# Products with the states on quarters of TensorE's array, tokens in chunk order, and writes issued by GpSimd

## The chip, the cores and the metric

The kernel runs on one core of a Trainium2 chip. The metric is the time of one execution on the device, in microseconds; several executions are timed, and the median counts. One more execution is recorded by the hardware profiler, and all rows below come from it.

## The reference

A decoder trunk of two layers over 512 tokens with 2048 channels, all in f32. Layer one is a diagonal state-space layer (S5): the input is normalised and multiplied by `s5_w_in` into u and z (2048 channels each); each group of 16 channels of u drives 64 complex states; y is read from the states, goes through gelu, a gate `sigmoid(y @ w_glu + b)` and `silu(z)`, then through `w_out` and a norm into the residual. Layer two is attention with forget gates over 16 heads. The change lies in layer one:

```python
bu = einsum('bsgc,gpc->bsgp', u, b)            # 128 groups of 16 channels, 64 complex states
h_t = abar * h_{t-1} + coef * bu_t             # scan over the 512 tokens
y = einsum('bsgp,gcp->bsgc', h_re, c_re) - einsum('bsgp,gcp->bsgc', h_im, c_im) + d * u
y = gelu(y);  y = y * sigmoid(y @ w_glu + b_glu) * silu(z)
h = x + rmsnorm(y @ w_out)
```

## The kernel before

Large products are made in split precision: each operand is a rounded part (`whi`, `ah`, `BH`) and a rest (`wlo`, `al`, `BL`), and three products of these parts are summed (`mm3`, lines 170 to 172). `proj` makes one block of 128 output channels for all 512 tokens from 48 such instructions. The weights of the next block are loaded while one runs (`ahead`, `piece`, line 145): a load of 512 KB into `wraw` (four buffers), the rounded part on ScalarE, the rest on VectorE. In layer one GpSimd issues these loads.

**Phase A** (`phase_a`) makes u and z, block by block, and between the blocks the state-space work. The order is written out by hand in `order_a`. The 512 tokens are cut into 64 chunks (`NC`) of 8 tokens (`CL`). For each block j of 128 channels, that is 8 groups of 16 channels, there are these steps, and here one block's steps are called a round:

- `ssm_u`: u is scaled by `rstd` on VectorE and written in the order (token in chunk, chunk). Eight DMAs on SP's queue write it to a scratch tensor `ub`, and one reads it back as `U`, with (channel, token in chunk) on the partitions.
- `ssm_tables`, `ssm_kernel`: tables are built from powers of the decay. The table `Et` of the output side makes, with `bb`, the small kernel `kps` (32 columns of the array for each of four pairs of groups). It goes to a scratch tensor `kd`, and eight DMAs on SP's queue read it as the banded matrices `M`, one for each group.
- `ssm_scan`: `xps` is the drive of each chunk from `U`; the scan runs on VectorE over the 64 chunks. Its result is written twice into `Hbd`, the states at the chunk starts, in block-diagonal form: the upper 64 partitions hold the even group and the lower 64 the odd one, each with zeros in the columns of the other.
- `ssm_y`: y of the chunk is the sum of two kinds of product in one bank, `yps`. First the states: for each of four pairs of groups and for the real and the imaginary part, one product of the whole array, 128 rows by 128 columns, with 128 moving columns, half of which are zeros of `Hbd` (line 526). Then the tokens: for each of eight groups and each half of the array's columns, one product with `M`, 128 rows by 64 columns, with 64 moving columns (line 531). Then gelu on ScalarE, and eight DMAs on SP's queue write y to `y_d`.

An f32 product appears in the trace as two instructions, each with its own weight load. The z blocks go to `z_d` by a DMA that ScalarE issues. The input of phase A is `xT`, x transposed on the host, and `rows` spreads `rstd` over the partitions.

**Phase B** reads y and z again, makes the gate with `w_glu`, and multiplies. z is in the order of the tokens and y in the order (token in chunk, chunk), so the product of the two reads z through a transposed view (`nat`, `tk`). Phases C to E hold `w_out`, the norm, and the attention layer.

The framework keeps order on each engine and adds the waits between engines; instructions marked urgent (`high_priority`), the loads of weights among them, are put earlier in an engine's queue.

Of the kernel before, what the change touches and what calls it, by code (L numbers as in the profile page):

```python
# [11 lines left out]
F32 = mybir.dt.float32  # L12
F32R = mybir.dt.float32r
I32 = mybir.dt.int32
AF = mybir.ActivationFunctionType
ALU = mybir.AluOpType
# [4 lines left out]
P = 128  # L21
S = 512
NQ = 4
CL = 8
NC = S // CL
# [39 lines left out]
class Kern:  # L65
# [226 lines left out]
                self.stt(y, a, 1.5, y, ALU.add, ALU.mult)  # L292
        return y

    def rows(self, r, out, pool, tag):

        nc = self.nc
        nb = S // P
        rb = pool.tile([P, nb, P], F32, tag=tag, name="rs_b", bufs=2 if tag == "ev" else 1)
        with self.tc.high_priority():  # L300
            nc.vector.tensor_copy(rb, r.unsqueeze(2).to_broadcast([P, nb, P]))
        ps = self.bank(name="rows")
        for b in range(nb):
            nc.tensor.matmul(ps[:, b * P:(b + 1) * P], lhsT=rb[:, b, :], rhs=self.ident, start=True, stop=True)
        self.act(out, ps)


# [133 lines left out]
    def ssm_kernel(self, j, T):  # L441

        nc, sp = self.nc, self.sp
        ql = NQ * (j % 4)
        qs = slice(NQ * j, NQ * j + NQ)

        Et = T["E"] = sp.tile([P, NQ, CL + 1, 16, 2], F32, tag="Et", name="Et", bufs=2)
        ev = Et.rearrange("p q t c s -> p q t (c s)")
        bc = [P, NQ, CL + 1, 32]
        pe = lambda c: self.AP[:, c, qs, :].unsqueeze(3).to_broadcast(bc)  # L450
        ve = lambda s: self.C4[s][:, ql:ql + NQ].unsqueeze(2).to_broadcast(bc)
        t = sp.tile(bc, F32, tag="tmp", name="ett")
        self.tt(ev, pe(0), ve(0), ALU.mult)
        self.tt(t, pe(1), ve(1), ALU.mult)
        self.tt(ev, ev, t, ALU.add)
        bb = self.bb[j % 2]
        for h in range(2):
            ph = slice(64 * h, 64 * h + 64)
            self.act(bb[ph, :, :, h, :], self.B4[ph, ql:ql + NQ, 1:3])

        kps = self.bank(name="kps")[:, :P]
        for q in range(NQ):
            for c in range(2):
                nc.tensor.matmul(kps[32 * q:32 * q + 32, :], lhsT=bb[:, q, c].rearrange("p g c -> p (g c)"),
                                 rhs=Et[:, q, 0:CL, :, c].rearrange("p t c -> p (t c)"),
                                 start=(c == 0), stop=(c == 1))
        kt = self.ktp[j % 2]
        self.stt(kt[:, 112:P], self.eye16, self.vec["d"][:, j:j + 1], kps[:, :16], ALU.mult, ALU.add)
        self.act(kt[:, P:240], kps[:, 16:])
        kd = self.dp.tile([8, 16, 240], F32, tag="kd", name="kd", bufs=2)  # L470
        nc.sync.dma_start(kd.rearrange("g c n -> (g c) n"), kt)
        M = T["M"] = sp.tile([P, 8, P], F32, tag="M", name="M", bufs=2)
        for g in range(8):
            s = kd[g]
            nc.sync.dma_start(M[:, g, :], bass.AP(s.tensor, s.offset, [[240, 16], [16, 8], [1, P]]))

    def ssm_u(self, j, ps):

        nc, sp = self.nc, self.sp
        u = sp.tile([P, CL, NC], F32, tag="u", name="u", bufs=2)  # L480
        self.tt(u.rearrange("p t k -> p k t"), ps.rearrange("p (k t) -> p k t", t=CL),
                self.rstd.rearrange("p (k t) -> p k t", t=CL), ALU.mult)
        ub = self.dp.tile([16, CL, 8, NC], F32, tag="ub", name="ub", bufs=2)
        for t in range(CL):
            nc.sync.dma_start(ub[:, CL - 1 - t].rearrange("c g k -> g c k"), u[:, t, :])
        U = sp.tile([P, 8, NC], F32, tag="U", name="U", bufs=3)
        nc.sync.dma_start(U, ub.rearrange("c t g k -> (c t) g k"))
        return U

    def ssm_scan(self, j, U, T):  # L490
# [21 lines left out]
        W = sp.tile(bc, F32, tag="Z", name="hw")  # L512
        self.tt(t, rot[:, :, ::2], G[:, :, ::-1], ALU.mult)
        self.tt(W, G, c_, ALU.mult)
        for h in range(2):
            ph = slice(64 * h, 64 * h + 64)
            self.tt(self.Hbd[ph, :, :, h, 1:], W[ph, :, :, :NC - 1], t[ph, :, :, :NC - 1], ALU.add)

    def ssm_y(self, j, U, T):
        nc, sp = self.nc, self.sp  # L520
        yps = self.bank(name="yps").rearrange("p (g k) -> p g k", k=NC)
        H, Et, M = self.Hbd, T["E"], T["M"]
        for q in range(NQ):
            o = yps[:, 2 * q:2 * q + 2, :].rearrange("p g k -> p (g k)")
            for c in range(2):
                nc.tensor.matmul(o, lhsT=Et[:, q, 1:CL + 1, :, c].rearrange("p t c -> p (t c)"),  # L526
                                 rhs=H[:, q, c].rearrange("p g k -> p (g k)"), start=(q == c == 0), stop=False)
        for g in range(2 * NQ):
            for h in range(2):
                ph = slice(64 * h, 64 * h + 64)  # L530
                nc.tensor.matmul(yps[ph, g, :], lhsT=M[:, g, ph], rhs=U[:, g, :],  # L531
                                 start=False, stop=(g == 2 * NQ - 1))

        g_ = sp.tile([P, 8, NC], F32, tag="gy", name="gy", bufs=2)
        self.act(g_, yps, AF.Gelu_apprx_tanh)
        for g in range(8):
            nc.sync.dma_start(self.y_d[j][g].rearrange("c t k -> t c k"), g_[:, g, :])

    def silu2(self, out, z):

# [62 lines left out]
    def phase_a(self, i):  # L603
        nc, K, D, tc = self.nc, self.K, self.D, self.tc
        self.NG = NQ * K
        with ExitStack() as ctx:
# [19 lines left out]
            self.dec = [sp.tile([P, NQ, 2, NC], F32, name=f"dec{b}") for b in range(2)]  # L626
            self.bb = [sp.tile([P, NQ, 2, 2, 16], F32, name=f"bb{b}") for b in range(2)]
            self.ktp = [sp.tile([P, 240], F32, name=f"ktp{b}") for b in range(2)]
            self.Hbd = sp.tile([P, NQ, 2, 2, NC], F32, name="hbd")
            for t in self.dec + self.bb + self.ktp + [self.Hbd]:  # L630
                nc.vector.memset(t, 0.0)
            hk = min(8, K)
            q4 = min(4, K)
# [53 lines left out]
            for n, (c, j) in enumerate(seq):  # L687
# [7 lines left out]
                if (c, j) == ("z", K - 1):  # L695
                    self.z_last = ps
                elif c == "z":
                    z = sp.tile([P, S], F32, tag="zt", name="zt", bufs=2)
                    self.act(z, ps)
                    (nc.sync if n < 2 else nc.scalar).dma_start(self.z_d[j], z)  # L700
                elif c == "u":
                    if j == 0:
                        self.rows(rstd, self.rstd, sp, "gt")
                    U[j] = self.ssm_u(j, ps)
                elif c == "tab":
                    T[j] = self.ssm_tables(i, j)
                elif c == "ker":
                    self.ssm_kernel(j, T[j])
                elif c == "scan":
                    self.ssm_scan(j, U[j], T[j])  # L710
                elif c == "y":
                    self.ssm_y(j, U[j], T[j])
# [30 lines left out]
    def phase_b(self, i, yh, yl):  # L743
# [5 lines left out]
        for f in range(K):  # L749
# [3 lines left out]
            self.tt(z, z, self.rstd, ALU.mult)  # L753
            self.act(t1, z, AF.Tanh, scale=0.5)
            self.stt(z, t1, 1.0, z, ALU.add, ALU.mult)
            self.tt(tk(y), nat(z), tk(y), ALU.mult)
            ps = self.proj(("g", f), yh, yl)
            th = tp.tile([P, S], F32, tag="t1", name="gth", bufs=2)
            self.act(th, ps, AF.Tanh, scale=0.5, bias=hb[:, f:f + 1])
# [326 lines left out]
def layouts(inp):  # L1086

    g = {k: np.ascontiguousarray(np.asarray(v)) for k, v in inp.items()}
    D = g["x"].shape[-1]
# [10 lines left out]
        return v.reshape(K, P).T  # L1100
    a = {}
    a["x"] = g["x"][0]
    a["xT"] = c(g["x"][0].T).reshape(K, P, S)
    a["w_in"] = wt(g["s5_w_in"][0])
    a["w_glu"] = wt(g["s5_w_glu"][0])
    a["w_out"] = wc(g["s5_w_out"][0])
# [47 lines left out]
```

## Time and profile before

| | |
|---|---|
| median of 3 runs | 1796.65 us (1795.36 to 1800.24) |
| profiled execution | 1793.25 us |
| its span, first to last instruction | 1791.5 us |
| TensorE busy in the span | 1772.2 us |
| VectorE, ScalarE, GpSimd busy | 1100.7, 588.9, 345.3 us |

Times in the trace are microseconds from the span's start. PE is TensorE's matmul, PEld its weight load, DVE VectorE, ACT ScalarE, POOL GpSimd, SP the engine that issues most DMAs; a q behind the name is that engine's queue of DMA issues. In a timeline, instructions of one kind that follow each other stand in one row, with their number; a matmul's duration there holds the time to drain, which overlaps the next one, so the pace of a row is read from its start and the start of the row behind it.

### The profile page before, as it was taken

The numbers are of one execution on the slowest core, as the hardware profiler recorded it, in microseconds if no ns is written. First come the engines' busy times: TensorE is split into PE (matmuls) and PEld (weight loads), VectorE is DVE, ScalarE is ACT, GpSimd is POOL, SyncE is SP. The second block draws the span as 40 slices with busy tenths as digits, with TensorE's granted clock in tenths as the row PEclk, the third lists the DMA queues.
The fourth block names the chain that finished last, engine by engine and source line by source line (L and its number), as shares of the span: only waits on it lengthen the run. The fifth ranks groups of instructions, "written<-read, shape, count | busy, mean of one in ns | idle before, by whom it ended". The sixth has DMA issues, their size and how long they took to land.

```text
span 1791.5 us, 24986 instructions
## 1 busy us (share of the span) xinstructions
PE 1772.2 (99%) x9942; PEld 1504.9 (84%) x9942; DVE 1100.7 (61%) x1598; ACT 588.9 (33%) x977; POOL 345.3 (19%) x241
## 2 busy tenths in 40 slices
PE   9999999999999999999999999999999999999997
PEld 6888888888888888898888888888888888988887
DVE  9789899985765622356664666455654556552235
ACT  7333332322544322225332323232332333332221
POOL 1000000000100000012433433334333343300000
PEclk9999999999999999999999999999999999999999
DMA  9545555545644453343333322232233222235332
GB/s 325 152 136 154 142 153 147 150 144 163 213 148 149 160 190 102 98 135 119 95 89 95 90 94 89 93 99 89 89 93 97 91 96 88 89 118 176 98 113 97
DMA packets 141334, 226.49 MB, mean 126 GB/s; under 512 B 53601, under 2 KB 80497, under 8 KB 140961
## 3 DMA queue, kind: packets, MB, share of 16 engines
q1 hardware_dynamic: 126000, 173.79, 31.4%
q0 software_dynamic: 13056, 47.33, 8.3%
q10 hardware_dynamic: 2160, 3.77, 0.6%
q8 instruction: 78, 1.28, 0.3%
q14 instruction: 40, 0.32, 0.1%
HBM read 201.88 MB, written 22.97 MB: 126 GB/s over the span
## 4 chain that ended last, share of the span: by engine, by line
PE 91%; DVE 4%; DMA 2%; SPq 1%; issue 0%; ACT 0%; DVEq 0%; ACTq 0%
PE proj L170 18%; PE proj L172 18%; PE proj L171 18%; PE tok L230 6%; PE tok L231 6%; PE tok L232 6%; PE v L205 3%; PE v L204 3%; PE v L206 3%; PE yps L526 1%; PE t L938 1%; PE yps L531 1%; PE xps L498 1%; DVE al L75 1%; PE btps L424 1%; DVE wlo L151 1%
## 5 line engine op out<-in xcount | busy, mean ns | idle before, releaser
L151 DVE TENSOR_TENSOR wlo<-wraw,whi 128x1024 fp32r<-128x1024 f32 x284 | 421.9, 1487 | 453.5 <-ACT whi L84 453.4
L84 ACT ACTIVATE whi<-wraw 128x1024 fp32r<-128x1024 f32 (+2 forms) x292 | 305.9, 1049 | 848.8 <-PE proj L172 508.2
L147 POOL TENSOR_TENSOR wraw<-wraw,vecs 128x1024 f32<-128x1024 f32 (+1 forms) x128 | 263.0, 2055 | 622.1 <-DMA wraw<-kv_k 254.8
L170 PE MATMUL proj<-BH,whi 128*128 128x512 f32 (+1 forms) x816 | 309.8, 380 | 0.0
L171 PE MATMUL proj<-BH,wlo 128*128 128x512 f32 (+1 forms) x816 | 307.7, 377 | 2.0 <-DVE wlo L151 2.0
L172 PE MATMUL proj<-BL,whi 128*128 128x512 f32 (+1 forms) x816 | 308.0, 377 | 0.5 <-DVE BL L72 0.5
L170 PE MATMUL proj<-ah,whi 128*128 128x512 f32 x768 | 302.2, 394 | 2.1 <-ACT zt L84 1.8
L171 PE MATMUL proj<-ah,wlo 128*128 128x512 f32 x768 | 299.4, 390 | 0.1
L172 PE MATMUL proj<-al,whi 128*128 128x512 f32 x768 | 299.1, 390 | 0.0
L171 PEld LDWEIGHTS proj<-BH,wlo 128*128 128x128 f32 x816 | 153.6, 188 | 30.2 <-DVE wlo L151 2.4
L172 PEld LDWEIGHTS proj<-BL,whi 128*128 128x128 f32 x816 | 153.5, 188 | 29.3 <-DVE BL L72 0.8
L170 PEld LDWEIGHTS proj<-BH,whi 128*128 128x128 f32 x816 | 153.6, 188 | 27.6
L170 PEld LDWEIGHTS proj<-ah,whi 128*128 128x128 f32 x768 | 144.1, 188 | 33.8 <-ACT zt L84 2.2
L171 PEld LDWEIGHTS proj<-ah,wlo 128*128 128x128 f32 x768 | 144.2, 188 | 30.4 <-DVE wlo L151 0.7
L172 PEld LDWEIGHTS proj<-al,whi 128*128 128x128 f32 x768 | 144.2, 188 | 30.3 <-DVE al L75 0.3
L205 PE MATMUL v<-wlo,BH 128*128 128x512 f32 (+2 forms) x320 | 111.4, 348 | 0.0
L204 PE MATMUL v<-whi,BH 128*128 128x512 f32 (+2 forms) x320 | 111.3, 348 | 0.0
L206 PE MATMUL v<-whi,BL 128*128 128x512 f32 (+2 forms) x320 | 111.3, 348 | 0.0
L230 PE MATMUL tok<-whi,BH 128*128 128x512 f32 (+1 forms) x320 | 111.1, 347 | 0.0
L230 PE MATMUL tok<-whi,ah 128*128 128x512 f32 (+1 forms) x320 | 111.0, 347 | 0.0
L232 PE MATMUL tok<-whi,al 128*128 128x512 f32 (+1 forms) x320 | 110.9, 347 | 0.0
L231 PE MATMUL tok<-wlo,ah 128*128 128x512 f32 (+1 forms) x320 | 110.9, 347 | 0.0
(211 smaller groups left out, 2359.9 us busy)
## 6 DMA issues: line engine op xcount, KB each, us to landing
wraw<-w_fox SPq DMA_DIRECT2D x64, 512.0 KB
wraw<-w_in POOLq DMA_DIRECT2D x58, 512.0 KB, 4.3
wraw<-w_glu POOLq DMA_DIRECT2D x32, 512.0 KB, 4.4
wraw<-w_out SPq DMA_DIRECT2D x32, 512.0 KB
wraw<-kv_k SPq DMA_DIRECT2D x32, 512.0 KB
wraw<-w_fo SPq DMA_DIRECT2D x32, 512.0 KB
wraw<-kv_v SPq DMA_DIRECT2D x28, 512.0 KB
M<-kd SPq DMA_DIRECT2D x128, 64.0 KB
```

Of the source, the lines that this page charges most:

```text
L84: self.nc.scalar.activation(out, in_, f, **kw)
L147: (eng or nc.vector).tensor_tensor(raw, raw, scale.unsqueeze(2).to_broadcast(shp), op=ALU.mult)
L151: (eng if eng and scale is None else nc.vector).tensor_tensor(lo, raw, hi, op=ALU.subtract)
L170: mm(ps, lhsT=hi, rhs=xh, start=(k == 0), stop=False)
L171: mm(ps, lhsT=lo, rhs=xh, start=False, stop=False)
L172: mm(ps, lhsT=hi, rhs=xl, start=False, stop=(k == self.K - 1))
L204: nc.tensor.matmul(o, lhsT=xh[k][:, bs], rhs=hi, start=(k == 0), stop=False)
L205: nc.tensor.matmul(o, lhsT=xh[k][:, bs], rhs=lo, start=False, stop=False)
L206: nc.tensor.matmul(o, lhsT=xl[k][:, bs], rhs=hi, start=False, stop=(k == K - 1))
L230: nc.tensor.matmul(ps, lhsT=xh[k][:, bs], rhs=hi, start=(k == 0), stop=False)
L231: nc.tensor.matmul(ps, lhsT=xh[k][:, bs], rhs=lo, start=False, stop=False)
L232: nc.tensor.matmul(ps, lhsT=xl[k][:, bs], rhs=hi, start=False, stop=(k == K - 1))
```

## The change

- `ssm_y`: the products with M come first. The products with the states are cut into quarters of the array: 64 rows (the partitions of an even or an odd group) by 64 columns (four of the eight tokens of a chunk), with 64 moving columns. Even groups go to one bank and odd groups to another, so there are 32 state products in place of 8. gelu is two instructions, one for each bank.
- `ssm_scan`: the states are written once, without the zeros, into `H`.
- `ssm_kernel`: the loop over the real and imaginary part is outside the one over the strips.
- Tokens are in the order (token in chunk, chunk) from the start of phase A: the host writes `xT` so, `rows` writes `rstd` so, and u, z and y need no transposed view on the way. `ub` is written with one DMA and read in pieces.
- The writes of y, and those of z but the first two and the last, are issued by GpSimd.

```diff
--- before.py
+++ after.py
@@ -292,7 +292,7 @@
                 self.stt(y, a, 1.5, y, ALU.add, ALU.mult)
         return y
 
-    def rows(self, r, out, pool, tag):
+    def rows(self, r, out, pool, tag, chunked=False):
 
         nc = self.nc
         nb = S // P
@@ -302,6 +302,8 @@
         ps = self.bank(name="rows")
         for b in range(nb):
             nc.tensor.matmul(ps[:, b * P:(b + 1) * P], lhsT=rb[:, b, :], rhs=self.ident, start=True, stop=True)
+        if chunked:
+            out, ps = out.rearrange("p (t k) -> p t k", t=CL), ps.rearrange("p (k t) -> p t k", t=CL)
         self.act(out, ps)
 
 
@@ -459,8 +461,8 @@
             self.act(bb[ph, :, :, h, :], self.B4[ph, ql:ql + NQ, 1:3])
 
         kps = self.bank(name="kps")[:, :P]
-        for q in range(NQ):
-            for c in range(2):
+        for c in range(2):
+            for q in range(NQ):
                 nc.tensor.matmul(kps[32 * q:32 * q + 32, :], lhsT=bb[:, q, c].rearrange("p g c -> p (g c)"),
                                  rhs=Et[:, q, 0:CL, :, c].rearrange("p t c -> p (t c)"),
                                  start=(c == 0), stop=(c == 1))
@@ -478,13 +480,12 @@
 
         nc, sp = self.nc, self.sp
         u = sp.tile([P, CL, NC], F32, tag="u", name="u", bufs=2)
-        self.tt(u.rearrange("p t k -> p k t"), ps.rearrange("p (k t) -> p k t", t=CL),
-                self.rstd.rearrange("p (k t) -> p k t", t=CL), ALU.mult)
-        ub = self.dp.tile([16, CL, 8, NC], F32, tag="ub", name="ub", bufs=2)
-        for t in range(CL):
-            nc.sync.dma_start(ub[:, CL - 1 - t].rearrange("c g k -> g c k"), u[:, t, :])
+        tk = lambda v: v.rearrange("p (t k) -> p t k", t=CL)
+        self.tt(u[:, ::-1], tk(ps), tk(self.rstd), ALU.mult)
+        ub = self.dp.tile([8, 16, CL, NC], F32, tag="ub", name="ub", bufs=2)
+        nc.sync.dma_start(ub.rearrange("g c t k -> (g c) t k"), u)
         U = sp.tile([P, 8, NC], F32, tag="U", name="U", bufs=3)
-        nc.sync.dma_start(U, ub.rearrange("c t g k -> (c t) g k"))
+        nc.sync.dma_start(U, ub.rearrange("g c t k -> (c t) g k"))
         return U
 
     def ssm_scan(self, j, U, T):
@@ -512,29 +513,33 @@
         W = sp.tile(bc, F32, tag="Z", name="hw")
         self.tt(t, rot[:, :, ::2], G[:, :, ::-1], ALU.mult)
         self.tt(W, G, c_, ALU.mult)
-        for h in range(2):
-            ph = slice(64 * h, 64 * h + 64)
-            self.tt(self.Hbd[ph, :, :, h, 1:], W[ph, :, :, :NC - 1], t[ph, :, :, :NC - 1], ALU.add)
+        self.tt(self.H[:, :, :, 1:], W[:, :, :, :NC - 1], t[:, :, :, :NC - 1], ALU.add)
 
     def ssm_y(self, j, U, T):
         nc, sp = self.nc, self.sp
-        yps = self.bank(name="yps").rearrange("p (g k) -> p g k", k=NC)
-        H, Et, M = self.Hbd, T["E"], T["M"]
+
+
+        yps = [self.bank(name=f"yps{h}")[:, :NQ * NC].rearrange("p (q k) -> p q k", k=NC) for h in range(2)]
+        H, Et, M = self.H, T["E"], T["M"]
+        half = [slice(64 * x, 64 * x + 64) for x in range(2)]
         for q in range(NQ):
-            o = yps[:, 2 * q:2 * q + 2, :].rearrange("p g k -> p (g k)")
+            for h in range(2):
+                for x in half:
+                    nc.tensor.matmul(yps[h][x, q], lhsT=M[:, 2 * q + h, x], rhs=U[:, 2 * q + h, :],
+                                     start=(q == 0), stop=False)
+        for q in range(NQ):
             for c in range(2):
-                nc.tensor.matmul(o, lhsT=Et[:, q, 1:CL + 1, :, c].rearrange("p t c -> p (t c)"),
-                                 rhs=H[:, q, c].rearrange("p g k -> p (g k)"), start=(q == c == 0), stop=False)
-        for g in range(2 * NQ):
-            for h in range(2):
-                ph = slice(64 * h, 64 * h + 64)
-                nc.tensor.matmul(yps[ph, g, :], lhsT=M[:, g, ph], rhs=U[:, g, :],
-                                 start=False, stop=(g == 2 * NQ - 1))
+                for n, x in enumerate(half):
+                    for h, ph in enumerate(half):
+                        nc.tensor.matmul(yps[h][x, q],
+                                         lhsT=Et[ph, q, 1 + 4 * n:5 + 4 * n, :, c].rearrange("p t c -> p (t c)"),
+                                         rhs=H[ph, q, c], start=False, stop=(q == NQ - 1 and c == 1))
 
         g_ = sp.tile([P, 8, NC], F32, tag="gy", name="gy", bufs=2)
-        self.act(g_, yps, AF.Gelu_apprx_tanh)
+        for h in range(2):
+            self.act(g_[:, h::2], yps[h], AF.Gelu_apprx_tanh)
         for g in range(8):
-            nc.sync.dma_start(self.y_d[j][g].rearrange("c t k -> t c k"), g_[:, g, :])
+            nc.gpsimd.dma_start(self.y_d[j][g].rearrange("c t k -> t c k"), g_[:, g, :])
 
     def silu2(self, out, z):
 
@@ -626,8 +631,8 @@
             self.dec = [sp.tile([P, NQ, 2, NC], F32, name=f"dec{b}") for b in range(2)]
             self.bb = [sp.tile([P, NQ, 2, 2, 16], F32, name=f"bb{b}") for b in range(2)]
             self.ktp = [sp.tile([P, 240], F32, name=f"ktp{b}") for b in range(2)]
-            self.Hbd = sp.tile([P, NQ, 2, 2, NC], F32, name="hbd")
-            for t in self.dec + self.bb + self.ktp + [self.Hbd]:
+            self.H = sp.tile([P, NQ, 2, NC], F32, name="hst")
+            for t in self.dec + self.bb + self.ktp + [self.H]:
                 nc.vector.memset(t, 0.0)
             hk = min(8, K)
             q4 = min(4, K)
@@ -697,10 +702,10 @@
                 elif c == "z":
                     z = sp.tile([P, S], F32, tag="zt", name="zt", bufs=2)
                     self.act(z, ps)
-                    (nc.sync if n < 2 else nc.scalar).dma_start(self.z_d[j], z)
+                    (nc.sync if n < 2 else nc.gpsimd).dma_start(self.z_d[j], z)
                 elif c == "u":
                     if j == 0:
-                        self.rows(rstd, self.rstd, sp, "gt")
+                        self.rows(rstd, self.rstd, sp, "gt", True)
                     U[j] = self.ssm_u(j, ps)
                 elif c == "tab":
                     T[j] = self.ssm_tables(i, j)
@@ -753,7 +758,7 @@
             self.tt(z, z, self.rstd, ALU.mult)
             self.act(t1, z, AF.Tanh, scale=0.5)
             self.stt(z, t1, 1.0, z, ALU.add, ALU.mult)
-            self.tt(tk(y), nat(z), tk(y), ALU.mult)
+            self.tt(y, z, y, ALU.mult)
             ps = self.proj(("g", f), yh, yl)
             th = tp.tile([P, S], F32, tag="t1", name="gth", bufs=2)
             self.act(th, ps, AF.Tanh, scale=0.5, bias=hb[:, f:f + 1])
@@ -1100,7 +1105,7 @@
         return v.reshape(K, P).T
     a = {}
     a["x"] = g["x"][0]
-    a["xT"] = c(g["x"][0].T).reshape(K, P, S)
+    a["xT"] = c(g["x"][0].T.reshape(D, NC, CL).transpose(0, 2, 1)).reshape(K, P, S)
     a["w_in"] = wt(g["s5_w_in"][0])
     a["w_glu"] = wt(g["s5_w_glu"][0])
     a["w_out"] = wc(g["s5_w_out"][0])
```

## Rows read from the trace of the kernel before

**Rows 1.** The page: busy time of the engines, and TensorE's granted clock in 40 slices.

```profile
PE 1772.2 (99%) x9942; PEld 1504.9 (84%) x9942; DVE 1100.7 (61%) x1598; ACT 588.9 (33%) x977; POOL 345.3 (19%) x241
...
PEclk9999999999999999999999999999999999999999
```

**Rows 2.** Busy time by stretch: engine busy (instructions), clock, DMA share, GB/s.

```profile
66.00:434.00 368.00, 366.98 (x2870) 308.43 (x2868) 320.06 (x359) 115.84 (x195) 27.06 (x52) 1.00 0.52 146
434.00:607.00 173.00, 173.00 (x767) 143.26 (x764) 103.20 (x116) 73.19 (x90) 16.21 (x31) 1.00 0.52 170
```

**Rows 3.** Timeline of TensorE, 113.9 to 119.3 us: start, us, engine, line, operation, tiles.

```profile
114.36 0.71 PE L464 MATMUL kps<-Et,bb 128*32 128x128 f32 x16
115.01 2.15 PE L526 MATMUL yps<-hbd,Et 128*128 128x128 f32 x16
117.08 1.15 PE L531 MATMUL yps<-U,M 128*64 128x64 f32 x32
118.07 1.10 PE L498 MATMUL xps<-U,BT 128*64 128x64 f32 x32
119.10 0.50 PE L170 MATMUL proj<-ah,whi 128*128 128x512 f32 x1
```

**Rows 4.** Timeline of TensorE, 129.8 to 136 us.

```profile
130.12 1.04 PE L424 MATMUL btps<-ident,Bt 128*128 128x128 f32 x8
130.99 2.04 PE L526 MATMUL yps<-hbd,Et 128*128 128x128 f32 x16
132.97 1.15 PE L531 MATMUL yps<-U,M 128*64 128x64 f32 x32
134.05 0.69 PE L464 MATMUL kps<-Et,bb 128*32 128x128 f32 x16
```

**Rows 5.** Timeline of TensorE from 399.6 us on; idle time and its releaser in brackets.

```profile
399.67 0.69 PE L464 MATMUL kps<-Et,bb 128*32 128x128 f32 x16
...
413.31 2.04 PE L526 MATMUL yps<-hbd,Et 128*128 128x128 f32 x16
415.29 0.45 PE L531 MATMUL yps<-U,M 128*64 128x64 f32 x8
416.51 1.09 PE L531 MATMUL yps<-U,M 128*64 128x64 f32 x16 [0.77 <-DMA M<-kd]
...
418.25 0.69 PE L464 MATMUL kps<-Et,bb 128*32 128x128 f32 x16
```

**Rows 6.** Timeline of TensorE, only what began or ran from 114.30 to 114.42 us.

```profile
114.36 0.35 PE L464 MATMUL kps<-Et,bb 128*32 128x128 f32 x4
```

**Rows 7.** Timeline of SP's queue, 396 to 418 us: start, us in all, line, tiles.

```profile
403.36 2.42 SPq L537 DMA_DIRECT2D y_d<-gy  x4
...
408.86 0.40 SPq L471 DMA_DIRECT2D kd<-ktp  x1
410.65 5.38 SPq L475 DMA_DIRECT2D M<-kd  x8
```

**Rows 8.** Groups of VectorE by line and shape, 66 to 607 us: busy us, mean ns.

```profile
L72 DVE TENSOR_TENSOR hbd<-hw,ht 64x504 f32<-64x504 f32 x32 | 21.7, 678 | 0.8
...
L72 DVE TENSOR_TENSOR u<-proj,rstd 128x512 f32<-128x512 f32 x16 | 17.3, 1081 | 1.9 <-PE proj L172 1.9
L72 DVE TENSOR_TENSOR yld<-zld,yld 128x512 f32<-128x512 f32 x14 | 16.0, 1141 | 0.5
...
L72 DVE TENSOR_TENSOR hw<-G,rot 128x512 f32<-128x512 f32 x16 | 11.0, 685 | 0.0
```

**Rows 9.** A group of GpSimd by line and shape, 0 to 900 us.

```profile
L145 POOL DMA_DIRECT2D wraw<-w_in x58 | 30.7, 530 | 382.9 <-DVE wlo L151 340.5 <-DMA xin<-xT 17.9 <-DVE scr L72 11.8
```

**Rows 10.** Timelines of GpSimd (first row) and of ScalarE (second), 200 to 232 us.

```profile
201.09 0.53 POOL L145 DMA_DIRECT2D wraw<-w_in  x1 [4.85 <-DVE wlo L151]
...
230.70 1.05 ACT L84 ACTIVATE whi<-wraw 128x1024 fp32r<-128x1024 f32 x1
```

**Rows 11.** Weight loads from GpSimd (line 145), 66 to 607 us.

```profile
DMA to landing us min/median/max: 3.8/4.3/7.2
```

## The prediction

> **What bounds the kernel now.** I read the page's busy shares first, then the busy time by stretch, then the timeline of TensorE around one round of the state-space stage, then the queues. [...]
>
> [...] In a round with a z projection before it, TensorE runs kps (114.36), the products of the states (115.01), those of the tokens with M (117.08), xps (118.07), and is back at a projection at 119.10 [rows 3]. In the other kind the order is btps, states, M, kps [rows 4]. From the first state product to the instruction after the last M product it is 118.07 - 115.01 = 3.06 us in the one and 134.05 - 130.99 = 3.06 us in the other. Sixteen of these are 49 us: that is what the change works on. One round differs: at 415.29 the M products stop for loads of M, and the part takes 418.25 - 413.31 = 4.94 us, 1.88 more [rows 5].
>
> **What the products cost, and what quarters may do.** An f32 product stands in the trace as two instructions. On the whole array with 128 columns streamed, btps takes (130.99 - 130.12)/8 = 0.109 us for each [rows 4], so 64 columns alone would take about 0.054. The state products take (132.97 - 130.99)/16 = 0.124, some with a change of shape in it. The M products, on 64 columns of the array with 64 streamed, take (118.07 - 117.08)/32 = 0.031 [rows 3]: half of 0.054 and a little, so the two halves of the array run side by side. kps, on strips of 32 columns with 128 streamed, takes 0.65/16 = 0.041 against 0.109, so strips overlap there as well, although the loop sends four instructions in a row to one strip.
>
> *Removed:* 16 instructions on the whole array (8 products), half of whose moving columns are zeros. *Added:* 32 products, 64 instructions, of 64 rows, 64 columns and 64 streamed. If the four quarters run side by side as the two halves do, a set of four takes what a pair of M instructions takes, 0.99/16 = 0.062 us, and 16 sets take 0.99 us. Changes of shape: the M part takes 0.99 us when the next work has its shape and 134.05 - 132.97 = 1.08 when it has not [rows 4], so about 0.09 for a change. After the edit M and states each end in one: 1.08 + 1.08 = 2.16 us. Round by round, kps to projection was 4.74 us and becomes 0.65 + 1.08 + 1.08 + 1.03 = 3.84. The saving is 0.90 us, and 16 × 0.90 = 14.4 us.
>
> No row of before shows an instruction on 64 rows, so its pace is bounded. Best: sets at 0.062 with no cost of shape, M and states 0.99 each, 1.08 saved, 17.3 us in all. Worst: no overlap at all, 64 × 0.054 = 3.46 us. I take the four side by side: halves and strips both overlap in this trace, and even and odd groups write to a bank each.
>
> How fast instructions can start also matters: 64 in 0.99 us is one each 0.015 us. The window that ends at 114.42 holds four kps instructions that began at 114.36 or later [rows 6], so starts can follow each other within about 0.02 us. That is a burst; whether it holds over 64 no row shows. [...]
>
> **The other edits.** *M ahead of the states:* in the late round M must now be there at 413.31, not 415.29 [rows 5]. But kd waited on SP's queue behind eight y writes and was issued at 408.86, although its kps had begun at 399.67 [rows 5] and takes 0.65; M's eight loads were issued from 410.65 on over 5.4 us [rows 7]. With y off that queue, kd can go out a few us after kps, some 5 us earlier, and M is there by about 411 to 413. I count the 1.88 us as gained; bounds: 0, or, with M no earlier, 2 us more lost, since the state products no longer cover it. *ub:* eight writes become one and U is read in pieces instead; U is loaded two rounds ahead, and the one us that TensorE is not busy in the stretch [rows 2] is the wait for M. *Order of kps:* strips overlap already; four at full pace would be 16 × 0.109/4 = 0.44 us plus a change of shape, at best 0.12 × 16 = 1.9 us; I take 0. *VectorE:* u 1081 ns and yld 1141 ns go to about 685, as the same shape without a transposed order takes, and two H sums of 678 become one [rows 8]: some 24 us less, none of it on the path, since TensorE is full in both stretches [rows 2]. If that cover were gone, it would be worth at most the few us of TensorE's waits. *ScalarE:* one gelu becomes two of half the size, at most as much again; its banks are next needed a projection later. The transposed write of rstd happens once.
>
> *y and z on GpSimd:* per round eight issues of y and mostly one of z. A weight load, with 128 rows like a write of y, costs 530 ns to issue [rows 9], so a round adds 9 × 0.53 = 4.8 us, plus a wait for gelu, in front of the weight loads queued behind. Who waits for those: whi, then wlo, then TensorE. There are four buffers, so the load issued at 201.09 is converted only after the three others, at 230.70 [rows 10], and it lands 4.3 us after issue, at most 7.2 [rows 11]. That leaves some 22 us, or, if the weight loads of the next product are queued strictly behind y, a few us. I count 0. On the last round y goes out after gelu as before, and SP is free for the loads of yld sooner.
>
> **The sum.** 14.4 + 1.9 = 16.3 us. The profiled execution took 1793.25 us (span 1791.5), so it would be 1777. The median shown is 1796.65, 3.4 above it; there the sum gives 1780.4, and I predict 1780. Some 0.3% (5.4 us) is what a measurement of this kernel can tell from no change.
>
> **Rivals.**
> *Two at a time.* Rows 0 to 63 and 64 to 127 of the same columns exclude each other, or the 0.031 us of an M instruction is the pace of issue and not of two halves. Then the states take 64 × 0.031 = 1.98 us plus 0.09, with M 3.15 against 3.06: 1.4 us lost over 16 rounds, 1.9 gained in the late one: 1796. For: kps and M both come near 0.03 to 0.04. Against: the four starts [rows 6]. Chance 0.16.
> [...] Chance 0.05. [...]
> *Quarters one by one (slower).* Place: the state products alone; price: 3.46 + 1.08 + 0.09 = 4.63 against 3.06, 1.57 × 16 = 25 us lost, 1.9 gained: 1820. It decides as soon as one of the 64 takes over 0.031 us. Against it: halves overlap with the same kind of instruction. Chance 0.06.
> *Weights late behind y.* It decides where GpSimd's extra 4.8 us a round, with the wait for gelu, grows past what the buffers leave, which needs about 1 us an issue and a strict order; 3 us lost in each second round is 24 us, 16 gained: about 1804. Chance 0.05.
>
> **How the numbers follow.** Four side by side has 0.68; its own range is 1775 (best shape costs and kps at its best) to 1786 (M's wait not gained, and 0.25 us more a round for shapes). Below it nothing is left. Two at a time reaches to 1797, and up to there 0.89 is held; the range 1775 to 1797 holds about 0.85 once I allow for mis-sized terms. Faster by over 0.3%: 0.68 + 0.05 = 0.73. Same: 0.16. Slower: 0.11.
>
> **What would show it.** In the timeline, states after M, 64 instructions in about 1.0 us; M and states 2.1 to 2.2 us in all rounds, the one at 413 without a wait; kps still 0.6 us; nine issues a round on GpSimd with no TensorE wait for wlo. VectorE's busy time falls by some 24 us without an effect of its own. It is wrong if the 64 take 2 us or more, if M's loads show among TensorE's waits, or if weights do.

## The result and the profile after

The changed kernel takes 1786.9 us, median of five runs (1782.97 to 1789.21), against 1796.05 of the kernel before on the same chip: ratio 0.9946, 95% interval 0.9935 to 0.9958. That is 9.2 us gained where 16.3 were forecast, inside the range. The profiled execution took 1786.9 us, its span 1785.1, so in the two profiles the spans differ by 6.4 us.

First the page of the changed kernel: busy time of the engines and the granted clock [rows 1].

```profile
PE 1762.5 (99%) x10710; PEld 1493.7 (84%) x10710; DVE 1078.4 (60%) x1582; ACT 590.1 (33%) x993; POOL 430.0 (24%) x382
...
PEclk9999999999999999999999999999999999999999
```

TensorE has 768 instructions more (16 rounds × 48) and is busy for 9.7 us less; VectorE 22.3 us less, GpSimd 84.7 us more. The timeline of TensorE in a round with a z projection [rows 3], and the busy time by stretch [rows 2], show where:

```profile
114.79 0.67 PE L466 MATMUL kps<-Et,bb 128*32 128x128 f32 x16
115.39 1.15 PE L528 MATMUL yps<-U,M 128*64 128x64 f32 x32
116.47 1.19 PE L534 MATMUL yps<-hst,Et 64*64 64x64 f32 x64
117.59 1.15 PE L499 MATMUL xps<-U,BT 128*64 128x64 f32 x32
118.67 0.50 PE L170 MATMUL proj<-ah,whi 128*128 128x512 f32 x1
```

```profile
66.00:422.00 356.00, 354.21 (x3644) 294.88 (x3643) 303.87 (x343) 116.53 (x211) 106.38 (x182) 1.00 0.54 153
...
805.00:870.00 65.00, 59.17 (x412) 55.75 (x411) 37.98 (x75) 21.51 (x42) 19.21 (x10) 0.95 0.26 82
```

The M part takes 116.47 - 115.39 = 1.08 us and the 64 state instructions 117.59 - 116.47 = 1.12, one each 0.0175 us: 2.20 us in place of 3.06. This repeats in all rounds to within 0.01 us, but for the last one. The round that waited for M [rows 5] now has no wait. From the start of the product that spreads `rstd` (65.51 us before, 66.34 after) to the end of the last round (434.02 and 421.77), the state-space stage shrinks from 368.51 to 355.43 us, by 13.1.

The last row of the windows is new to the argument: between 805 and 870 us, in the attention layer, whose code the change does not touch, TensorE is busy for 59.17 of 65 us, and the mean granted clock is 0.95. In the kernel before, the same stretch of the program lies some 12 us later and loses less:

```profile
817.00:882.00 65.00, 60.74 (x445) 57.22 (x444) 39.99 (x77) 23.92 (x45) 20.89 (x11) 1.00 0.29 90
```

Of the 12.25 us by which TensorE is ahead at the end of the state-space stage, 11.5 are left at the first value product (tile `v`; 829.45 and 817.95), 7.96 at the cumulated gates (873.19 and 865.23), and 6.4 at the end of the span. Where the last 1.6 us go was not traced.

The other edits in the profile: groups of VectorE by line and shape [rows 8], and one of GpSimd, 66 to 607 us.

```profile
L72 DVE TENSOR_TENSOR u<-proj,rstd 128x512 f32<-128x512 f32 x16 | 11.0, 686 | 3.3 <-PE proj L172 3.3
L72 DVE TENSOR_TENSOR hst<-hw,ht 128x504 f32<-128x504 f32 x16 | 10.9, 683 | 0.6
```

```profile
L542 POOL DMA_DIRECT2D y_d<-gy x128 | 76.7, 606 | 15.9 <-ACT gy L84 4.3 <-issue 3.9 <-DMA y_d<-gy 3.5
```

### The profile page after: what moved, and what is told of

The parts are those of the page before. It is cut to its first block, busy times and chain, and to the rows that moved or that the text cites. A ratio compares the mean times of both kernels' runs of the same rounds, so it can differ in the third digit from the quotient of the medians.

```text
span 1785.1 us, 26466 instructions
## 1 busy us (share of the span) xinstructions
PE 1762.5 (99%) x10710; PEld 1493.7 (84%) x10710; DVE 1078.4 (60%) x1582; ACT 590.1 (33%) x993; POOL 430.0 (24%) x382
## 3 DMA queue, kind: packets, MB, share of 16 engines
q0 software_dynamic: 18192, 55.01, 10.3%
## 4 chain that ended last, share of the span: by engine, by line
PE 92%; DVE 5%; DMA 2%; issue 1%; ACT 0%; SPq 0%; POOL 0%; DVEq 0%; ACTq 0%; POOLq 0%
PE proj L170 18%; PE proj L172 18%; PE proj L171 18%; PE tok L232 6%; PE tok L231 6%; PE tok L230 6%; PE v L204 3%; PE v L205 3%; PE v L206 3%; PE yps L534 1%; PE t L943 1%; PE yps L528 1%; PE xps L499 1%; DVE wlo L151 1%; PE btps L426 1%; DVE al L75 1%
```

## The experiments

Each ratio is against the kernel before, run beside it on the same chip (its medians were 1795.2 to 1796.3 us); "stage" is the time from the `rstd` product to the end of the last round in the profiled execution (368.5 before, 355.4 changed). A time is the median of four or five runs of the kernel, of twelve and eleven for the two under 1.

### 1. The products alone, and the rest alone

`q_only` is the kernel before with the product change only: quarters, two banks, M first, states written once, two gelu. Queues, token order and kps are as before. `rest_only` is the changed kernel with the old products, whole array with `Hbd` and one bank; the ends of its edit, with the old loops of `ssm_y` between them:

```diff
-        self.tt(self.H[:, :, :, 1:], W[:, :, :, :NC - 1], t[:, :, :, :NC - 1], ALU.add)
+        for h in range(2):
+            ph = slice(64 * h, 64 * h + 64)
+            self.tt(self.Hbd[ph, :, :, h, 1:], W[ph, :, :, :NC - 1], t[ph, :, :, :NC - 1], ALU.add)
...
-        for h in range(2):
-            self.act(g_[:, h::2], yps[h], AF.Gelu_apprx_tanh)
+        self.act(g_, yps, AF.Gelu_apprx_tanh)
```

> Only the products: states on quarters in two banks, M first, one H; tokens, queues and the order of kps as in the kernel before. Theory 1 (the gain is the shorter state products): a round's M and state part falls from 3.06 to about 2.2 us, in all rounds but the late one, some 13 us by the end of the state-space stage; y is still ahead of kd on SP's queue, so the late round waits for M for 2 to 4 us. Time 0.4 to 0.7% under before. Theory 2 (the gain is mostly the freed queues and vector work): under 0.2% better than before.

> All of the change but the products: states as before, on the whole array with the zeros, in one bank, ahead of M. Theory 1: the 16 rounds keep 3.06 us each, only the wait for M in the late round goes, so the time is within 0.2% of before. Theory 2: most of the 9 us are here, 0.4% better or more.

Measured: q_only 1796.21 us, ratio 1.0001 (0.999 to 1.0011); stage 366.2. rest_only 1792.39, ratio 0.9988 (0.9979 to 0.9997); stage 365.6. In q_only the products are as short as in the changed kernel, 1.08 and 1.12 us, but three rounds wait for M: the M part takes 2.70, 7.68 and 3.00 us there. So the trace bears out the mechanism of theory 1, with more waits than it allowed for, although the time is the one that theory 2 gave. Timeline of TensorE in the second of these, and of SP's queue ahead of it:

```profile
405.39 0.34 PE L527 MATMUL yps<-U,M 128*64 128x64 f32 x4
409.00 1.59 PE L527 MATMUL yps<-U,M 128*64 128x64 f32 x20 [3.28 <-DMA M<-kd]
411.85 0.48 PE L527 MATMUL yps<-U,M 128*64 128x64 f32 x4 [1.25 <-DMA M<-kd]
412.65 0.48 PE L527 MATMUL yps<-U,M 128*64 128x64 f32 x4 [0.32 <-DMA M<-kd]
```

```profile
395.70 2.51 SPq L541 DMA_DIRECT2D y_d<-gy  x4
398.39 0.32 SPq L487 DMA_DIRECT2D U<-ub  x1
398.75 2.43 SPq L541 DMA_DIRECT2D y_d<-gy  x4
401.28 0.40 SPq L471 DMA_DIRECT2D kd<-ktp  x1
403.07 5.08 SPq L475 DMA_DIRECT2D M<-kd  x8
```

The eight writes of y stand ahead of kd, and M is still on its way when its products begin. The x20 instructions of the second row take (411.85 - 1.25 - 409.00)/20 = 0.08 us each where 0.034 is usual, and the granted clock was 0.56 on average from 409 to 412 us. So neither part saves much alone: the shorter products are eaten by the queue, and a free queue has only the one wait of before to remove.

### 2. Which of the queue's loads matters

`queues_back` is the changed kernel with y on SP and z on ScalarE again; u still goes out in one write. `q_and_y` is q_only with y and z on GpSimd, and still eight writes of `ub` and the old token order. The edit of queues_back (that of q_and_y is its reverse, on q_only):

```diff
-            nc.gpsimd.dma_start(self.y_d[j][g].rearrange("c t k -> t c k"), g_[:, g, :])
+            nc.sync.dma_start(self.y_d[j][g].rearrange("c t k -> t c k"), g_[:, g, :])
...
-                    (nc.sync if n < 2 else nc.gpsimd).dma_start(self.z_d[j], z)
+                    (nc.sync if n < 2 else nc.scalar).dma_start(self.z_d[j], z)
```

> The changed kernel with the writes of y issued by SP again and those of z by ScalarE; u still goes through one write and the products stay on quarters. Theory: y ahead of kd on SP's queue makes M late, and that eats the shorter products. Then kd and M are issued some 4 to 5 us later in the late rounds, TensorE waits for M in at least one of the last three rounds, 3 us or more in all (with the clock lowered behind a long wait perhaps more), the state-space part ends 3 to 9 us later than in the changed kernel (421.8 us), and the time is 1790 to 1796 us. Rival: the eight writes of ub were what blocked SP; then the stage ends by about 423 and the time stays at 1786 to 1788.

> The kernel before with the quarters (M first, two banks, states written once, two gelu) and with y and z issued by GpSimd, but with the eight writes of ub and the token order of before. Theory (y's queue is what matters): no long wait for M, the state-space part ends by 421 to 424 us, the time is 1784 to 1789 us, as the changed kernel's. Rival (the eight writes of ub, or the transposed reads on VectorE, count too): M is late again, the part ends at 427 or later and the time is 1791 to 1796 us.

> The changed kernel once more, on the same chip as the three others, so that they can be compared with it; 1785 to 1789 us. If the wait at the z0 product depends on which of the two engines begins first, it may be about 2 us this time in place of 3.9, with no fall of the clock there, and the span 3 us shorter; if the chain itself got longer, it is 3.9 again.

Measured: queues_back 1787.84 us, ratio 0.9959 (0.9947 to 0.9972), stage 360.8; q_and_y 1784.68, ratio 0.9936 (0.9924 to 0.9949), stage 355.8; the changed kernel once more 1786.22, ratio 0.995 (0.9936 to 0.9963), stage 355.5. In queues_back the last two rounds wait for M, and the M part takes 4.16 and 3.50 us there; its timeline:

```profile
402.82 0.80 PE L528 MATMUL yps<-U,M 128*64 128x64 f32 x20
406.37 0.68 PE L528 MATMUL yps<-U,M 128*64 128x64 f32 x12 [2.74 <-DMA M<-kd]
406.98 1.65 PE L534 MATMUL yps<-hst,Et 64*64 64x64 f32 x64
```

The stage is 5.3 us longer there, as the theory of y's queue said; the time, 1.6 us longer, is less than it said (1790 to 1796), and the two intervals overlap. With y gone, the eight writes of `ub` cost nothing: q_and_y has the stage of the changed kernel within 0.4 us and its time within the interval. So, beside the quarters, only the move of y and z is needed. No run moves one of the two alone; the queue in the rows above holds y and no z. The single write of `ub`, the token order and the shorter work on VectorE add nothing that shows.

### 3. The order of the quarters

`by_quarter` sends the same 32 state products, one quarter's eight after the other's:

```diff
-        for q in range(NQ):
-            for c in range(2):
-                for n, x in enumerate(half):
-                    for h, ph in enumerate(half):
+        for n, x in enumerate(half):
+            for h, ph in enumerate(half):
+                for q in range(NQ):
+                    for c in range(2):
```

> The changed kernel with the 32 state products sent quarter by quarter, eight in a row (16 instructions) to each. If TensorE takes work for a free quarter from behind waiting instructions, as it seems to do with the strips of kps, the states stay at about 1.1 us a round and the time is that of the changed kernel. If instructions start in the order in which they are sent, each quarter runs alone: 64 at 0.055 to 0.06, some 3.6 us a round, 40 us more in all, slower than before.

Measured: 1821.55 us, ratio 1.0144 (1.0131 to 1.0157). Timeline of TensorE:

```profile
115.44 1.15 PE L528 MATMUL yps<-U,M 128*64 128x64 f32 x32
116.53 3.50 PE L534 MATMUL yps<-hst,Et 64*64 64x64 f32 x64
119.96 0.74 PE L499 MATMUL xps<-U,BT 128*64 128x64 f32 x18
```

The states take 119.96 - 116.53 = 3.43 us, 0.0536 each: near the price of "no overlap at all" in the prediction (3.46), and its slower rival to 2 us (1820). So the gain comes from four quarters at work at once, and here that needed an order that goes round them: 1.12 us for the states in place of 3.43.

That 3.43 is so near to 3.46 is luck. Within one quarter an instruction starts each 0.060 us, so 64 without any overlap would take 3.84; but two quarters overlap where one takes over from the other. The rows are windows of TensorE's timeline, inside the first quarter (117.16 to 117.18 us) and at the border to the second (117.46 to 117.48):

```profile
117.00 0.40 PE L534 MATMUL yps<-hst,Et 64*64 64x64 f32 x4
117.30 0.40 PE L534 MATMUL yps<-hst,Et 64*64 64x64 f32 x7
```

Four starts in 0.18 us become seven. In all 16 rounds the second quarter begins 0.774 to 0.778 us after the first, where sixteen starts of the first alone would need more than 0.95: three of its sixteen are still to come. So, by these starts, three waiting instructions are passed, but not the fifteen and more that this order would need. It fits that kps overlapped for the most part in the kernel before, with four in a row to each strip: 16 instructions in 0.61 to 0.65 us, where one after the other at the 0.109 of btps would be 1.74 [rows 3, 4].

### 4. States ahead of M

`states_first` swaps the two loops of `ssm_y` back, with the quarters kept:

```diff
-            for h in range(2):
-                for x in half:
-                    nc.tensor.matmul(yps[h][x, q], lhsT=M[:, 2 * q + h, x], rhs=U[:, 2 * q + h, :],
-                                     start=(q == 0), stop=False)
-        for q in range(NQ):
...
-                                         rhs=H[ph, q, c], start=False, stop=(q == NQ - 1 and c == 1))
+                                         rhs=H[ph, q, c], start=(q == c == 0), stop=False)
+        for q in range(NQ):
+            for h in range(2):
+                for x in half:
+                    nc.tensor.matmul(yps[h][x, q], lhsT=M[:, 2 * q + h, x], rhs=U[:, 2 * q + h, :],
+                                     start=False, stop=(q == NQ - 1))
```

> The changed kernel with the states ahead of M again. If a change of shape costs 0.09 us, M is followed by xps in its own shape in the 8 rounds with a z projection: 0.8 us less; the last round's wait for M (1.1 us in the changed kernel) is covered by the states. 1 to 2 us better in the state-space stage, which the time can hardly tell. If M first was needed for the overlap or for the bank, it gets slower instead.

> The changed kernel with the state products ahead of those with M, once more, as the base of the other two: 1780 to 1784 us.

Measured: 1782.13 us, ratio 0.9925 (0.9913 to 0.9936), and again 1782.42, ratio 0.9919 (0.9906 to 0.9933); stage 352.2 both times. It beats both kernels. Timeline of TensorE in a round with a z projection:

```profile
115.94 1.19 PE L529 MATMUL yps<-hst,Et 64*64 64x64 f32 x64
117.06 1.15 PE L535 MATMUL yps<-U,M 128*64 128x64 f32 x32
118.04 1.10 PE L499 MATMUL xps<-U,BT 128*64 128x64 f32 x32
119.08 0.50 PE L170 MATMUL proj<-ah,whi 128*128 128x512 f32 x1
```

M takes 118.04 - 117.06 = 0.98 us, 0.10 less, since xps behind it has its shape, and xps itself takes 119.08 - 118.04 = 1.04, 0.05 less by the unrounded times. There are seven such rounds. In the eight with btps ahead, btps keeps its 0.97. The last round does not wait for M, because the states cover 1.12 us of its way. That is 7 × 0.15 + 1.12 = 2.2 of the 3.2 us by which the stage is shorter; the other 1.05 us are the stall told at the end of this document, which is gone as well.

### 5. What was lost behind the stage

The second profile of the changed kernel (`after_again`) has the same stage within 0.1 us, but a span of 1781.2 us, 3.9 shorter. Most of the difference, some 3.2 us, is in the first z product of the attention layer (z0). Another 0.7 us were lost at 810 us: behind a wait of 1.69 us the granted clock was 0.50 from 810 to 813 us in the first profile, and it did not fall there in the second. TensorE at z0 in the first profile, and in the second:

```profile
857.03 0.28 PE L170 MATMUL proj<-BH,whi 128*128 128x256 f32 x1
860.90 0.58 PE L171 MATMUL proj<-BH,wlo 128*128 128x256 f32 x1 [3.60 <-DVE wlo L151]
861.28 0.41 PE L172 MATMUL proj<-BL,whi 128*128 128x256 f32 x1
861.50 0.41 PE L170 MATMUL proj<-BH,whi 128*128 128x256 f32 x1
...
864.27 0.29 PE L171 MATMUL proj<-BH,wlo 128*128 128x256 f32 x1
864.40 0.28 PE L172 MATMUL proj<-BL,whi 128*128 128x256 f32 x1
```

```profile
856.85 0.28 PE L170 MATMUL proj<-BH,whi 128*128 128x256 f32 x1
858.80 0.39 PE L171 MATMUL proj<-BH,wlo 128*128 128x256 f32 x1 [1.67 <-DVE wlo L151]
859.02 0.28 PE L172 MATMUL proj<-BL,whi 128*128 128x256 f32 x1
859.14 0.28 PE L170 MATMUL proj<-BH,whi 128*128 128x256 f32 x1
```

What VectorE and GpSimd do at that moment, first profile:

```profile
857.92 2.92 DVE L151 TENSOR_TENSOR wlo<-wraw,whi 128x1024 fp32r<-128x1024 f32 x1
...
857.87 1.90 POOL L147 TENSOR_TENSOR wraw<-wraw,vecs 128x1024 f32<-128x1024 f32 x1 [5.45 <-DMA wraw<-w_fox]
```

and second:

```profile
857.53 1.22 DVE L151 TENSOR_TENSOR wlo<-wraw,whi 128x1024 fp32r<-128x1024 f32 x1
...
857.51 2.98 POOL L147 TENSOR_TENSOR wraw<-wraw,vecs 128x1024 f32<-128x1024 f32 x1 [6.02 <-DMA wraw<-w_fox]
```

GpSimd's multiply of the next weights and VectorE's `wlo` begin within 0.05 us of each other, and one of them is stretched by nearly the length of the other: 2.92 in place of 1.22, or 2.98 in place of 1.90. Which one loses decides whether TensorE waits 3.87 us from start to start or 1.95. Behind the longer wait the clock falls: from 861.28 to 864.27 TensorE's instructions follow each other at 0.214 us in place of 0.120, and the windows give a granted clock of 0.50:

```profile
857.00:861.00 4.00, 0.41 (x4) 0.20 (x2) 3.97 (x5) 0.63 (x1) 1.90 (x1) 0.98 0.03 11
861.00:864.00 3.00, 3.00 (x14) 3.00 (x15) 0.45 (x1) 0.00 (x0) 0.00 (x0) 0.50 0.55 173
```

That costs 14 × 0.094 = 1.3 us more. (In q_only the clock fell behind a wait of 2.05 us as well, to 0.53 on average from 870 to 873 us.) Over the eleven profiles that share this code, the start of `wlo` against that of the multiply goes with which of the two is stretched; why, no run shows. In six VectorE keeps its 1.22 us: there `wlo` begins between 184 ns ahead of the multiply and 12 ns behind it (both of the kernel before, rest_only, q_only, after_again, states_first), and TensorE's wait is 1.86 to 2.17 us from start to start. In five GpSimd keeps its 1.90 us: there `wlo` begins 51 to 121 ns behind (the changed kernel's first, q_and_y, queues_back, by_quarter, sf_again), and the wait is 3.65 to 3.87.

`no_scale` leaves GpSimd's multiply out (the attention layer's weights are used unscaled); `sf_vec5` and `sf_vec` are states_first with VectorE multiplying, for five products or for all. The first edit below is that of no_scale, the second that of sf_vec5; sf_vec has `self.stream(items)` there:

```diff
-            if scale is not None:
+            if scale is not None and eng is None:
...
-        self.stream([w + (nc.gpsimd,) for w in items])
+        self.stream([w if n < 5 else w + (nc.gpsimd,) for n, w in enumerate(items)])
```

> The changed kernel without GpSimd's multiply of the attention layer's weights (the pieces are used unscaled, so the output is another one). Theory: that multiply, when it begins before VectorE's wlo, holds wlo up (2.92 in place of 1.22 us), and this with the granted clock that falls behind the wait is what was lost between 805 and 870 us. Then all wlo of that stretch take about 1.2 us, the wait at the z0 product falls from 3.9 to about 2 us, the clock does not fall there, and the time is 1781 to 1784 us. Rival (the loss has nothing to do with the two engines; the wait comes from the chain of the forget gate on VectorE): the wait and the time stay, 1786 to 1788 us.

> States ahead of M, and VectorE in place of GpSimd multiplies the weights of the first five products of the attention layer (up to the one behind z0). Theory: two engines that hold each other up cost 4 us or more between 800 and 870 us, even in the run in which the wait at z0 was short. Then no wlo there takes over 1.4 us, the wait at z0 goes to 1 us or less, and the time is 1777 to 1780 us. Rival: each piece now passes VectorE twice, behind the chain of the forget gate, so wlo is late at z0 all the same, by 3 us or more with a fall of the clock behind it; then 1781 to 1786.

> As the one with the first five, but VectorE multiplies the weights of all products of the attention layer. Theory: TensorE is never without work from 870 to 1600 us, VectorE is busy for 58% of that stretch there and gets some 100 us more, so it makes no difference to the one with five: 1777 to 1780. Rival: with VectorE fuller, softmax or wlo come late and TensorE waits in that stretch: over 1785.

Measured: no_scale 1777.39 us, ratio 0.9901 (0.9888 to 0.9915), 8.8 us below the changed kernel beside it, with the same stage (355.1). TensorE's busy time from 805 to 870 us is

```profile
805.00:870.00 65.00, 63.94 (x462) 60.51 (x462) 33.88 (x86) 25.69 (x49) 1.29 (x1) 1.00 0.28 95
```

against 59.17 and, in the second profile, 60.67 us of the changed kernel. The wait at z0 is gone altogether, not only down to 2 us as expected; presumably the weights are also there earlier without the multiply, which was not traced. So this run shows what the multiply costs in all, and the pair of profiles above shows what the collision alone does.

Giving the multiply to VectorE takes the collision away only in sf_vec (from 795 to 870 us each `wlo` takes 1.22 to 1.29 us there, and in sf_vec5 one still takes 2.67), and makes another wait: sf_vec5 1787.81 us, ratio 0.9951 (0.9938 to 0.9963); sf_vec 1789.23, ratio 0.9958 (0.9945 to 0.997); 5.4 and 6.8 us slower than states_first beside them, and for sf_vec5 above both ranges that I expected. Timeline of TensorE in sf_vec5:

```profile
808.52 1.94 PE L797 MATMUL hT<-ident,al 128*128 128x128 f32 x8 [4.23 <-DVE al L75]
...
847.88 0.74 PE L170 MATMUL proj<-BH,whi 128*128 128x512 f32 x1 [4.09 <-DVE ke L75]
```

The instructions that TensorE waits for on VectorE now come later than before: the first of these waits was 1.69 us in sf_again and the second is new. A lower granted clock stands behind each (0.50 from 808.5 to 812 us, 0.58 from 848 to 852), and together they cost more than the collision.

A second profile of the kernel before asked whether the long wait at z0 belongs to the change:

> The kernel before, unchanged, for a second profile of it. Theory: the wait at the z0 product is chance, about 2 or about 3.8 us whichever kernel runs, with a fall of the clock behind the long one; then this profile shows one of the two values, the state-space part takes 368.5 us from rows to its end within 0.5, and if the long wait is there the span is 1794 to 1796. Rival: the long wait belongs to the changed kernel; then it is 1.9 again and the span is 1791 to 1792.

Its span is 1795.7 us, 4.2 longer than the first, but not for z0: the wait there is 2.17 us from start to start, as short as in the first (1.86). The late round took longer, 4.53 us for its M part against 2.97, with a granted clock of 0.57 behind it, from 420 to 424 us, and the stage 371.6 us, not the 368.5 that I expected. So the kernel before has a luck of its own, at M.

## Why the prediction was right, and where it was off

- *Four quarters at once:* right. 64 instructions took 1.12 us; forecast was 1.08. Behind the first, the sets of four start each 0.060 us; forecast was 0.062. Two at a time (1.98 us) and one by one (3.46) are out, and by_quarter shows about what the latter would have looked like.
- *Whether close starts hold over 64:* they do, one each 0.0175 us with the start and the change of shape in it, in every round. The 0.05 that the prediction adds to 0.68 stands for a slower pace of starts; no run shows such a pace for instructions that go round four quarters at a granted clock of 1.00.
- *Changes of shape:* M and states take 2.20, forecast 2.16. Not counted was the change between btps and M: btps takes 130.68 - 129.71 = 0.97 us after and 0.87 before [rows 4]:

```profile
129.71 1.04 PE L426 MATMUL btps<-ident,Bt 128*128 128x128 f32 x8
130.68 1.15 PE L528 MATMUL yps<-U,M 128*64 128x64 f32 x32
```

  That is 0.10 lost in each second round. The sum also left xps at 1.03, the value behind M; behind the states it takes 118.67 - 117.59 = 1.08, 0.05 lost in seven rounds. The new order of kps, counted at nothing, gives 0.60 for 0.61 to 0.65. Summed over the stage in the two traces, btps is 0.74 us longer, xps 0.19 (one xps near the end got shorter) and kps 0.52 shorter: 0.4 us lost in all.
- *M's wait:* the 1.88 us of the late round were gained as forecast. But a round that did not wait before now does, the last one:

```profile
418.44 1.04 PE L528 MATMUL yps<-U,M 128*64 128x64 f32 x28
420.38 0.34 PE L528 MATMUL yps<-U,M 128*64 128x64 f32 x4 [0.91 <-DMA M<-kd]
420.64 1.19 PE L534 MATMUL yps<-hst,Et 64*64 64x64 f32 x64
```

  The M part takes 420.64 - 418.44 = 2.20 us, 1.12 too many. (In `after_again` the M part takes 2.70 there.) The step "M ahead of the states" named this price (2 us "since the state products no longer cover it") for the late round only. states_first shows that the new order of the two products was itself worth less than nothing.
- *Weights late behind y:* out. A write of y costs GpSimd 606 ns, more than the 530 counted, and TensorE waits for no weights in the stage.
- *VectorE's and ScalarE's work:* VectorE's busy time fell by 22.3 us (forecast some 24), and q_and_y, which keeps the transposed reads, is no slower.
- *The sum* is where the prediction was off, in its size. Over the stage it nearly holds: 16 × 0.86 + 1.88 - 1.12 = 14.5 us from M and states, less the stall of 1.05 told below and the 0.4 of btps, xps and kps, is 13.1, and 13.1 are there. But the prediction took it that what the stage gains arrives at the end, because TensorE is full behind it [rows 2]. That window ended at 607 us. From 805 to 870 TensorE waits for VectorE, and what it loses there is not a constant: two executions of the same program differ by 3.9 us in their spans. In the profiles of before the wait at z0 is the short one, twice; in the changed kernel the long one came in one of two, and in all profiles with the quarters whose attention layer is untouched, in five of eight. So part of the shortfall is chance: against the second profile of the changed kernel the first one of before is 10.3 us longer. Why `wlo` meets the multiply more closely in these kernels is not settled: in the two profiles of before it begins 122 and 184 ns ahead, in the changed kernel's 52 and 12 ns behind. A start of TensorE's work that is 0.8 us later in the profile after was not traced; it varied from 65.15 to 67.20 us over the kernels here.
- *The profiled execution and the median:* the sum was made against 1793.25 us, some 3 us under the median. The second profile of before (1797.47) shows why they differ: the wait for M in the late round was longer. That wait is part of what the change removes, so a typical execution may gain a little more in the stage than the first profiles showed. How often the long wait at z0 takes that back, two profiles of each kernel don't tell.

## What to carry to other kernels

A product whose operand is half zeros in blocks was worth cutting to quarters of the array here, with consecutive instructions going round the quarters: 1.12 us in place of 1.98 to 2.07 [rows 3, 4]. Sent quarter by quarter, at 3.43, it was slower than the zeros. Here each row half also had a bank of its own; whether that is needed, no run shows. When a product becomes shorter, look at the transfers that it covered: here the gain was nil (q_only, ratio 1.0001) until the writes of y left the queue in front of M's loads (q_and_y, 0.9936), and the part whose input comes later belongs last. A gain is the stage's until the later stages have been checked for waits: take a second profile of the same program, and where two engines' instructions that stretch each other begin as close as `wlo` and the multiply here, from 184 ns ahead to 121 ns behind, count both outcomes.

## What the runs showed of the hardware that was not expected

Instructions on 64 × 64 with 64 columns streamed, sent round four quarters, start in sets of four each 0.060 us, and one quarter alone in by_quarter starts one each 0.060: in the steady run the factor is 4. The whole parts compare as 1.12 to 3.43 us, a factor of 3.06, because the first set takes 0.11 us, a change of shape (0.09 us by M in rows 4) is in both, and the borders in by_quarter overlap. By this pace, three of a quarter's sixteen instructions still wait in by_quarter when the first of the next quarter starts, 0.774 to 0.778 us after its own first.

One projection of the changed kernel stands still for about 1 us with no wait that the profile shows. Timeline of TensorE in its first profile:

```profile
246.94 0.40 PE L171 MATMUL proj<-ah,wlo 128*128 128x512 f32 x1
248.22 0.39 PE L172 MATMUL proj<-al,whi 128*128 128x512 f32 x1 [0.88 <-issue]
```

From start to start that is 1.28 us, where 0.23 is usual. It came at the same place in both profiles of the changed kernel and in no_scale, q_and_y and queues_back (0.43 to 1.28 us), and not in by_quarter, q_only, rest_only, states_first or the kernel before. Its cause stays open.
